# Last two experts of a mixture layer added as late rows, three weight loads in flight to the end, bookkeeping at another place

## The chip, the cores and the metric

One core of one Trainium2 chip runs the kernel. The metric is the device time of one execution in microseconds, as the median of three runs. Engines are named as in the profile: PE (TensorE, PEld its weight loads), DVE (VectorE), ACT (ScalarE), POOL (GpSimd), SP (the engine that here only issues DMAs).

## The reference

One layer of a hybrid backbone on 512 latent tokens and 256 context tokens of width 1024: modulation from a conditioning vector, a bidirectional gated linear attention, and then a grouped top-2 mixture of 16 experts, and a final RMSNorm. The change lies in the last two parts:

```
h2 = modulate(rmsnorm(x, norm2_g), sh2, sc2)           # (512, 1024)
scores = sigmoid(h2 @ w_router);  sel = scores + b_router
best   = group (of 4) with the largest sum of its two largest sel
idx    = the two largest sel inside that group
gates  = one_hot(idx) * scores / (sum of the two scores)
for e in range(16):
    he  = silu(h2 @ w1[e]) * (h2 @ w3[e])              # 1024 -> 512
    out = out + gates[:, e] * (he @ w2[e])             # 512 -> 1024
x = x + g2 * out
return rmsnorm(x, final_g)
```

Every token goes to two experts of one group, so each expert has some of the 512 tokens.

## The kernel before

**Sparse experts.** The kernel counts and ranks the tokens of each expert on the chip. Experts 2 to 15 of its order are sorted by their number of tokens, so that slot 14 and 15 hold the smallest (room for 32 tokens each). Each expert is a tile of tokens: `Tile_` (over 64 tokens, products split in three terms), `Part` for 64 or 32 tokens, where 2 or 4 column groups of the array work side by side on a half or a quarter of the width (`A` = 4 for the last two). The tokens' rows are gathered from DRAM (`h2d`) by indirect DMA on POOL, and an expert's result is added to the rows of `accd` in DRAM by an indirect DMA that accumulates (`scatter`, line 1106). One such scatter waits for the one before it.

**Weights.** An expert's weights are six units of 1 MB: parts a and b (gate and up, line 688) and d (down). `pump` issues them on SP in the order of `queue`, as soon as a buffer is free; `load_unit` also makes each load wait until an earlier one has landed (`back`), which sets how many are in flight: 3, and 2 from the 88th load on and for the two halves of the last unit.

**Order.** The main loop, for i from 0 to 14, does up a of expert i, down of i-1, up b of i, and then the scatter of i-1. Its order on PE, DVE and ACT comes from the scheduler, POOL's is written. The tail (after `finish_consts`) is written out by hand for all engines: down of 14, its scatter, up of 15, reads of `accd` into four tiles of 128 tokens (line 1342), a gather of expert 15's own rows of `accd` (`late_rows`), then squares, norm and output of the four tiles (`finish_half`), the down product of 15, and its rows once more with expert 15's part added (`late_add`, `late_square`, `late_out`), which POOL stores over the output (`late_store`, line 1393).

**Bookkeeping.** A block behind that (`ctx2`, lines 1457 to 1491) works out which experts have more tokens than their room; a loop then treats those (`For_i`, with the number `nblk` read from SBUF). The scheduler may place the block on DVE from the mark of expert 10's store on.

Of the kernel before, what the change touches and what calls it, by code (L numbers as in the profile page):

```python
# [8 lines left out]
F32 = mybir.dt.float32  # L9
# [9 lines left out]
P = 128  # L19
# [13 lines left out]
def dit_kernel(ctx: ExitStack, tc: tile.TileContext, I, out):  # L33
# [647 lines left out]
    def load_unit(u, e, s, hs=None):  # L681
        t = u[s] if s in u else free.pop(0)
        if t is None:
            t = stg.tile([P, 2048], F32, tag="st", name="st")
        w, v = (I[("w_gate_e", "w_up_e")[s % 2]], s // 2) if s < 4 else (I["w_down_e"], s - 4)
        w = w[0, e, v] if isinstance(e, int) else w[0, bass.ds(e, 1), v].rearrange("a p n -> (a p) n")
        h = slice(0, 2048) if hs is None else slice(1024 * hs.start, 1024 * hs.stop)
        d = nc.sync.dma_start(t[:, h], w[:, h])
        if len(dmas) >= 3 and not isinstance(e, int):
            back = 2 if hs is not None or len(dmas) >= 88 else 3  # L690
            tc.add_manual_dep(d.ins, dmas[-back].ins.name, mybir.DependencyInfo(mybir.DependencyClass.Sync, mybir.DependencyReason.DATA), reason="queue depth")
        dmas.append(d)
        u[s] = t
# [488 lines left out]

    class Part:
        def __init__(s, c, w):
            s.idx, s.gs, s.late, s.mark = gix2[:, c:c + 1], gsl[:, c:c + 1], None, None
# [26 lines left out]
        def tr(s):  # L1212
            pt = bank(pb)
            for k in range(s.nk):
                PE.transpose(pt[:, k * P:(k + 1) * P], s.he[:, k * P:(k + 1) * P], ident)
            pt = pt[:, 0:s.n].rearrange("p (k a t) -> p k a t", k=s.nk, a=s.A)
            s.hr = s.he[:, 0:s.n // 2].rearrange("p (k a t) -> p k a t", k=s.nk, a=s.A // 2)
            S.activation(s.hr, pt[:, :, 0:s.A // 2], AF.Silu)
            V.tensor_mul(s.hr, s.hr, pt[:, :, s.A // 2:s.A])
            s.py = bank()[:, 0:s.n]  # L1220

        def dn(s, kt, w):
# [90 lines left out]
    one = raw2[0:1, :]  # L1313
    ss3, rstd3 = R("ss3", [4]), R("rstd3", [4])
    fin = {}

    def finish_consts():
        f, e = free.pop(0), free.pop(0)
        fin["g"], fin["j"], fin["row"] = f[:, 0:1024], f[:, 1024:2048], f[0:1, 1024:2048]
        fin["y"], fin["z"] = [[u[:, h * 1024:h * 1024 + 1024] for u in (free.pop(0), free.pop(0)) for h in range(2)] for _ in range(2)]  # L1320
        fin["h"], fin["g2"], fin["y15"] = [e[:, k * 512:k * 512 + 512] for k in range(3)]
        nc.scalar.dma_start(fin["row"], I["final_g"].rearrange("(o n) -> o n", o=1))
        V.memset(one, 1.0)
# [8 lines left out]
    def finish_g():  # L1332
        for a in range(2):
            sl = slice(a * 512, a * 512 + 512)
            pt = bank()
            PE.matmul(pt, one, fin["row"][:, sl], start=True, stop=True)
            S.copy(fin["g"][:, sl], pt)
        lay("h", fin["g"])
# [5 lines left out]
    def squares(t):  # L1344
        S.activation(fin["j"], fin["y"][t], AF.Square, accum_out=ss3[:, t:t + 1])

    def finish_rsqrt(t):
        rsqrt(rstd3[:, t:t + 2], ss3[:, t:t + 2], 2, 1.0 / D, "a", between=(lambda: finish_mul(3)) if t else None)

    def finish_mul(t):  # L1350
        (V if t % 2 else G).tensor_mul(fin["z"][t], fin["y"][t], fin["g"])

    def finish(t):
        z, r = fin["z"][t], rstd3[:, t:t + 1]
        V.tensor_scalar(z, z, r, None, op0=OP.mult)
# [12 lines left out]
    QA = P // tiles[-1][2]
    SELP = wr.rearrange("p k e -> p (k e)")
# [4 lines left out]
    lrs = R("lrs", [1])  # L1374

    def late_rows(t):
        t.z = xbuf()[:, 0:t.n]
        gather(t.z, parts(accd, t.A), t.idx, t.A * T)

    def late_add(t):  # L1380
        V.tensor_add(t.z, t.z, t.y)

    def late_square(t):
        S.activation(mo.tile([P, 512], BF16, tag="ohx", name="jk3", bufs=NO)[:, 0:t.n], t.z, AF.Square, accum_out=lss)

    def late_out(t):
# [34 lines left out]
    with tc.manual_schedule(engines=tail):  # L1421
        p_, q_ = ex[NE - 2:]
        p, q = p_.tls[0], q_.tls[0]
        p.late = mo.tile([P, D], F32, tag="t4", name="y", bufs=NY)[:, 0:p.n]
        q.late = fin["y15"][:, 0:q.n]
# [6 lines left out]
        for c in "uFab":  # L1432
            if c == "F":
                finish_load()
            elif c in "0123":
                finish_load([int(c)])
            else:
                load_unit(wts[NE - 1], regs[NE - 1], {"u": 4}.get(c, 5), {"a": range(1), "b": range(1, 2)}.get(c))
        late_rows(q)
        q_.turn()  # L1440
        S.preload_act_table_set("natural_log_exp_and_others")
        for h in range(2):
            finish_half(2 * h)
# [32 lines left out]
    t64 = big2[:, 0:64]  # L1476
    for x in range(NB):
        V.scalar_tensor_tensor(t64, cr, float(x + 1), capb.rearrange("p b e -> p (b e)"), op0=OP.is_equal, op1=OP.mult)
        V.tensor_reduce(off[:, x:x + 1], t64, axis=AX.X, op=OP.add)
        V.tensor_scalar(t64, cr, float(x + 1), None, op0=OP.is_equal)  # L1480
        V.tensor_reduce(ohe[:, x], t64.rearrange("p (b e) -> p e b", b=4), axis=AX.X, op=OP.add)
        ob = ohe[:, x].unsqueeze(1).to_broadcast([P, 4, NE])
        V.tensor_mul(tmp4.rearrange("p (t e) f -> p t (e f)", t=4), zm, ob)
        V.tensor_reduce(pmo[:, x], tmp4.rearrange("p (t e) f -> p t (e f)", t=4), axis=AX.X, op=OP.add)
        V.tensor_mul(tmp4.rearrange("p (t e) f -> p t (e f)", t=4), oh[:, 1], ob)
        V.tensor_reduce(k1o[:, x], tmp4.rearrange("p (t e) f -> p t (e f)", t=4), axis=AX.X, op=OP.add)
# [53 lines left out]
```

## Time and profile before

| | us |
|---|---|
| median of 3 runs (654.6 to 658.16) | 656.12 |
| the profiled execution | 656.5 |
| its span | 654.7 |
| busy PE / DVE / ACT / POOL | 599.0 / 463.6 / 302.6 / 98.3 |
| DMA traffic | 168.41 MB, mean 257 GB/s |

The profiled execution is one more run, 0.4 us above the median; the span goes from its first to its last instruction. Times in the rows are counted from the start of the span. A DMA's issue and its landing are two things: the row of the issuing engine shows the issue alone.

### The profile page before, as it was taken

Reading aid. Unit: us, or ns where it says so; the run is one execution under the profiler, and the core shown is the slowest. Engines: PE = TensorE matmul, PEld = TensorE weight load, DVE = VectorE, ACT = ScalarE, POOL = GpSimd, SP = SyncE. Lnnn points to the kernel's source line nnn. Section 1 sums busy time; section 2 is a strip of 40 time slices with the busy share of each in tenths; the row PEclk is TensorE's granted clock in tenths of the full one; section 3 lists DMA queues with packets and bytes.
Section 4 is the critical chain, followed back from the end, with each engine's and each line's share of the span. In section 5 each row is a group of like instructions: output and inputs, shape, how many; then the busy total and the mean of one; then the engine's idle time right before and its main releaser. Section 6 shows DMA issues by size and latency. Waiting matters only on the chain. (4 is left out here: it accounts for less than half of the span.)

```text
span 654.7 us, 11203 instructions
## 1 busy us (share of the span) xinstructions
PE 599.0 (91%) x4200; PEld 412.4 (63%) x4200; DVE 463.6 (71%) x984; ACT 302.6 (46%) x511; POOL 98.3 (15%) x102
## 2 busy tenths in 40 slices
PE   3999999999999999999979989999999999999741
PEld 2778577776878878778748465545565657664310
DVE  5667499849985972575288399465767689999615
ACT  6433399257352233642451255334444457773131
POOL 4030000010100010012200330120322222222032
PEclk9999999999999999999998999999999999999975
DMA  8996472220234861658662989899999999999974
GB/s 269 340 353 218 175 274 66 67 66 4 67 130 158 270 232 51 254 183 354 237 227 74 373 316 366 326 342 351 412 387 395 362 352 358 393 383 345 298 273 189
DMA packets 50251, 168.41 MB, mean 257 GB/s; under 512 B 6779, under 2 KB 17237, under 8 KB 37138
## 3 DMA queue, kind: packets, MB, share of 16 engines
q1 hardware_dynamic: 43216, 156.26, 64.4%
q0 software_dynamic: 5024, 8.70, 5.6%
q10 hardware_dynamic: 1954, 2.71, 1.3%
q8 instruction: 34, 0.56, 0.3%
q14 instruction: 23, 0.19, 0.1%
HBM read 158.64 MB, written 12.30 MB: 261 GB/s over the span
## 5 line engine op out<-in xcount | busy, mean ns | idle before, releaser
L51 PE MATMUL bk<-wh,fh 128*128 128x512 f32 (+3 forms) x276 | 110.9, 409 | 0.7 <-ACT fh L56 0.4
L52 PE MATMUL bk<-wl,fh 128*128 128x512 f32 (+3 forms) x276 | 111.3, 405 | 0.0
L53 PE MATMUL bk<-wh,fl 128*128 128x512 f32 (+3 forms) x276 | 109.0, 399 | 0.5 <-DVE fl L57 0.5
L282 DVE TENSOR_TENSOR wl<-st,wh 128x512 fp32r<-128x512 f32 x60 | 39.9, 685 | 38.9 <-ACT wh L281 37.6
L56 ACT CAST wh<-su 128x1024 fp32r<-128x1024 f32 x45 | 46.8, 1047 | 39.9 <-PE bk L53 38.7
L281 ACT CAST wh<-st 128x512 fp32r<-128x512 f32 x60 | 35.9, 620 | 59.5 <-PE bk L53 50.8
L51 PEld LDWEIGHTS bk<-wh,fh 128*128 128x128 f32 (+3 forms) x276 | 50.2, 183 | 19.2 <-ACT wh L56 3.3
L57 DVE TENSOR_TENSOR wl<-su,wh 128x1024 fp32r<-128x1024 f32 x45 | 54.5, 1222 | 10.5 <-ACT wh L56 8.3
L1106 POOL DMA_INDIRECT accd<-y,gix x16 | 37.2, 2324 | 164.8 <-DVE y L1166 78.2
L52 PEld LDWEIGHTS bk<-wl,fh 128*128 128x128 f32 (+3 forms) x276 | 50.6, 183 | 16.5 <-issue 3.3
L53 PEld LDWEIGHTS bk<-wh,fl 128*128 128x128 f32 (+3 forms) x276 | 50.6, 183 | 13.7 <-issue 1.2
L1202 PE MATMUL bk<-su,he 128*64 128x512 f32 (+1 forms) x136 | 21.7, 526 | 12.5 <-DMA su<-in_w_down_e_dram 9.6
L1202 PE MATMUL bk<-su,xg 128*32 128x256 f32 (+1 forms) x216 | 31.7, 485 | 1.5 <-DVE xg L1196 1.5
L56 ACT CAST fx<-su 128x1024 fp32r<-128x1024 f32 x21 | 22.0, 1050 | 21.8 <-PE bk L53 21.6
L57 DVE TENSOR_TENSOR fx<-su,fx 128x1024 fp32r<-128x1024 f32 x21 | 25.7, 1222 | 7.4 <-ACT fx L56 7.2
L51 PE MATMUL bk<-fx,fh 128*128 128x512 f32 (+3 forms) x68 | 27.9, 410 | 1.2 <-ACT fh L56 1.2
L52 PE MATMUL bk<-fx,fh 128*128 128x512 f32 (+3 forms) x68 | 27.3, 402 | 1.0 <-DVE fx L57 1.0
L53 PE MATMUL bk<-fx,fl 128*128 128x512 f32 (+3 forms) x68 | 26.6, 394 | 0.2 <-DVE fl L57 0.2
L1102 POOL DMA_INDIRECT xg<-h2d,gix x16 | 20.1, 1259 | 39.2 <-DVE pis L1005 15.1
L250 POOL DMA_DIRECT2D mrd<-mrow x8 | 3.8, 487 | 129.2 <-DVE mrow L248 129.2
L1202 PEld LDWEIGHTS bk<-su,he 128*64 128x64 f32 (+1 forms) x136 | 6.6, 127 | 24.4 <-DMA su<-in_w_down_e_dram 11.0
L57 DVE TENSOR_TENSOR fl<-bk,fh 128x512 fp32r<-128x512 f32 (+3 forms) x25 | 15.5, 634 | 7.5 <-ACT fh L56 5.5
(476 smaller groups left out, 1303.6 us busy)
## 6 DMA issues: line engine op xcount, KB each, us to landing
su<-in_w_up_e_dram SPq DMA_DIRECT2D x23, 1024.0 KB, 8.2
su<-in_w_down_e_dram SPq DMA_DIRECT2D x21, 1024.0 KB, 7.8
su<-in_w_gate_e_dram SPq DMA_DIRECT2D x19, 1024.0 KB, 8.3
st<-in_gla_w_in_dram SPq DMA_DIRECT2D x10, 1024.0 KB, 5.0
QQ<-in_w_mod_dram SPq DMA_DIRECT2D x5, 1024.0 KB, 10.8
st<-in_w_gate_e_dram SPq DMA_DIRECT2D x5, 1024.0 KB, 6.8
st<-in_w_up_e_dram SPq DMA_DIRECT2D x5, 1024.0 KB, 9.0
B<-in_w_mod_dram SPq DMA_DIRECT2D x4, 1024.0 KB, 5.1
```

Of the source, the lines that this page charges most:

```text
L51: PE.matmul(o, ah, bh, start=first, stop=False)
L52: PE.matmul(o, ah, bl, start=False, stop=False)
L53: return PE.matmul(o, al, bh, start=False, stop=last)
L56: S.copy(hi, full)
L57: return V.tensor_sub(lo, full, hi.bitcast(F32))
L250: G.dma_start(mrd[4 * h_ + c4:4 * h_ + c4 + 1, :], mrow[32 * c4:32 * c4 + 1, :])
L281: S.copy(w[0][:, k], st[:, k])
L282: mark[0] = V.tensor_sub(w[1][:, k], st[:, k], w[0][:, k].bitcast(F32))
L1102: G.indirect_dma_start(out=xg, out_offset=None, in_=src, in_offset=bass.IndirectOffsetOnAxis(ap=idx, axis=0), bounds_check=n - 1, oob_is_e ...
L1106: G.indirect_dma_start(out=dst, out_offset=bass.IndirectOffsetOnAxis(ap=idx, axis=0), in_=y, in_offset=None, bounds_check=n - 1, oob_is_er ...
L1202: PE.matmul(o[s.w * a:s.w * a + s.w], l, r(a), start=first, stop=last, tile_position=(0, s.w * a))
```

## The change

Six things are edited. (1) `back` is 3 everywhere. (2) Expert 14 is no longer scattered into `accd`: both 14 and 15 are late. `late_consts` makes two one-hot matrices (`hot`: which token of the four tiles stands in which row of the expert) and two matrices of equal numbers (`same`: which rows of the one expert are the same token as which rows of the other). `late_rows` picks the rows of `accd` out of the four tiles by products with `hot`, and `late_other` adds the other expert's share by a product with `same`. Both experts' rows are then normed and stored. (3) The final gain is loaded as a broadcast to 128 partitions, not as one row spread by two products. (4) An output tile is one fused DVE operation (`finish_out`), and POOL does no product. (5) Expert 15's gate uses Exp and a reciprocal (`by_exp`), so that the table is loaded earlier. (6) The bookkeeping may start at expert 4's mark, and its nine steps are done three at a time.

```diff
-            back = 2 if hs is not None or len(dmas) >= 88 else 3
+            back = 3
...
+            gate, up = pt[:, :, 0:s.A // 2], pt[:, :, s.A // 2:s.A]
+            if s.by_exp:
+                S.activation(s.hr, gate, AF.Exp, scale=-1.0)
+                V.tensor_scalar(s.hr, s.hr, 1.0, None, op0=OP.add)
+                V.reciprocal(s.hr, s.hr)
+                V.tensor_mul(s.hr, s.hr, gate)
...
-        nc.scalar.dma_start(fin["row"], I["final_g"].rearrange("(o n) -> o n", o=1))
+        nc.scalar.dma_start(fin["g"], I["final_g"].rearrange("(o n) -> o n", o=1).partition_broadcast(P))
...
-            PE.matmul(pt, one, fin["row"][:, sl], start=True, stop=True)
-            S.copy(fin["g"][:, sl], pt)
...
-    def finish_mul(t):
-        (V if t % 2 else G).tensor_mul(fin["z"][t], fin["y"][t], fin["g"])
-
-    def finish(t):
-        z, r = fin["z"][t], rstd3[:, t:t + 1]
-        V.tensor_scalar(z, z, r, None, op0=OP.mult)
+    def finish_out(t):
+        z = fin["y"][t]
+        V.scalar_tensor_tensor(z, z, rstd3[:, t:t + 1], fin["g"], op0=OP.mult, op1=OP.mult)
         nc.sync.dma_start(out[0, t * P:(t + 1) * P, :], z)
...
-    def late_rows(t):
-        t.z = xbuf()[:, 0:t.n]
-        gather(t.z, parts(accd, t.A), t.idx, t.A * T)
...
+    def late_consts(ts):
+        c = NTL - 2
+        V.tensor_copy(key, gix2[:, c:c + 2])
+        for k in range(2):
+            for t in range(4):
+                V.tensor_scalar(fin["hot"][k][:, t], iot[:, 0:32], zp[:, t, ND - 2 + k:ND - 1 + k], None, op0=OP.is_equal)
+            pt = bank(pb)[:, 0:P]
+            PE.transpose(pt, key[:, k:k + 1].to_broadcast([P, P]), ident)
+            V.tensor_scalar(fin["same"][k], pt, key[:, 1 - k:2 - k], None, op0=OP.is_equal)
+
+    def late_rows(ts, k):
+        for i, t in enumerate(ts):
+            if k == 0:
+                t.rows, t.z = bank()[:, 0:t.n], fin["late"][2 + i]
+            t.groups(t.rows, fin["hot"][i][:, k], lambda a: fin["y"][k][:, a * t.n:a * t.n + t.n], k == 0, k == 3)
+
+    def late_other(ts, i):
+        pt = bank()[:, 0:ts[i].n]
+        PE.matmul(pt, fin["same"][i], ts[1 - i].y, start=True, stop=True)
+        return pt
...
+        G.drain()
+        late_consts(pq)
         p_.down(wts[NE - 2])
-        p_.scatter()
-        G.drain()
-        finish_g()
+        S.preload_act_table_set("natural_log_exp_and_others")
         q_.up(wts[NE - 1], "a")
+        load_unit(wts[NE - 1], regs[NE - 1], 4)
+        finish_load()
+        for h in range(2):
+            load_unit(wts[NE - 1], regs[NE - 1], 5, range(h, h + 1))
+        S.copy(fin["late"][3], late_other(pq, 1))
         q_.up(wts[NE - 1], "b")
...
+        for k in range(2, 4):
+            squares(k)
+            late_rows(pq, k)
+        finish_scale(2)
+        lay("h", fin["g"])
+        V.tensor_add(p.z, p.y, p.rows)
+        V.tensor_add(q.z, q.z, q.rows)
+        finish_out(2)
         q_.down(wts[NE - 1])
-        late_add(q)
-        late_square(q)
-        late_out(q)
-        late_store(q)
+        V.tensor_add(q.z, q.z, q.y)
+        V.tensor_add(p.z, p.z, late_other(pq, 0))
+        finish_out(3)
+        late_out(pq)
...
-    ctx2.enter_context(tc.issue_after(ex[10].mark.ins))
+    ctx2.enter_context(tc.issue_after(ex[4].mark.ins))
```

On SP, before, the end of the weight loads and the reads of `accd`, with what each waits for (DMAHW and DMASW are landings of DMAs of SP or ACT and of POOL, by lanes; `su` and `st` are weight buffers, `B` and `su_2692` take the rows of `accd`):

```order
L688 DMA su_2700<-in_w_gate_e_dram 128x2048 [waits DMAHW6_49,PE_49]
L688 ISA
L688 DMA su_2693<-in_w_up_e_dram 128x2048 [waits DMAHW7_49,PE_49]
L688 ISA
L688 DMA st<-in_w_gate_e_dram 128x2048 [waits DMAHW2_49,DMAHW0_49,DVE_49]
L688 ISA
L688 DMA st<-in_w_up_e_dram 128x2048 [waits DMAHW3_49,DMAHW1_49,DVE_49]
L688 ISA
L688 DMA su_2698<-in_w_down_e_dram 128x2048 [waits DMAHW2_49,PE_49]
L1342 DMA B_86<-accd 128x1024 [waits DMASW7_49,DMASW6_49,DMASW0_49]
```

The same place on SP now:

```order
L688 DMA su_2700<-in_w_gate_e_dram 128x2048 [waits DMAHW5_49,PE_49]
L688 ISA
L688 DMA su_2693<-in_w_up_e_dram 128x2048 [waits DMAHW6_49,DMAHW1_49,PE_49]
L688 ISA
L688 DMA st<-in_w_gate_e_dram 128x2048 [waits DMAHW7_49,DVE_49]
L688 ISA
L688 DMA st<-in_w_up_e_dram 128x2048 [waits DMAHW0_49,DVE_49]
L688 ISA
L688 DMA su_2696<-in_w_down_e_dram 128x2048 [waits DMAHW1_49,PE_49]
L1341 DMA B_86<-accd 128x1024 [waits DMASW7_49,DMASW6_49,DMASW4_49]
```

Each load waits for the landing of the third load before it, not the second; the load into `su_2693` also waits for lane DMAHW1, on which the gain's broadcast stands; the read of `accd` waits for the scatters of 11 to 13, not for one of 14 (lane DMASW0).

On POOL, before, from the scatters of experts 12, 13 and 14 on:

```order
L1106 DMA accd<-y,gix 512x1024 [waits DMASW4_49,DVE_49]
L1106 DMA accd<-y,gix_3326 1024x512 [waits DMASW6_49,DVE_49]
L1106 DMA accd<-y,gix_3326 2048x256 [waits DMASW7_49,DVE_49]
L1102 DMA xg<-accd,gix_3326 128x256 [waits DMASW1_49,DMASW0_49,PE_49]
L1351 TENSOR_TENSOR su_2696<-B_86,srg 128x1024 [waits DMAHW6_49,DMAHW5_49,DMAHW7_49,DMAHW1_49,Activation_49]
L1351 TENSOR_TENSOR su_2697<-su_2692,srg 128x1024 [waits DMAHW3_49,DMAHW7_49,DMAHW0_49,PE_49]
L1393 DMA out_dram<-xg,gix_3326 2048x256 [waits DMAHW5_49,DMAHW4_49,DMAHW6_49,DMAHW3_49,DVE_49]
```

And now:

```order
L1102 DMA xg<-h2d,gix_3326 128x256 [waits DMASW7_49,PE_49]
L1106 DMA accd<-y,gix 512x1024 [waits DMASW4_49,DVE_49]
L1106 DMA accd<-y,gix_3326 1024x512 [waits DMASW6_49,DVE_49]
L1401 DMA out_dram<-srg,gix_3326 2048x256 [waits DMAHW5_49,DMAHW4_49,DMAHW6_49,DMAHW3_49,DVE_49]
L1401 DMA out_dram<-srg,gix_3326 2048x256 [waits DMASW1_49,DMASW0_49,DVE_49]
```

The third scatter, the gather and the two products are gone; there are two late stores, and the second waits for lane DMASW0, which is that of the first.

On DVE, now, from the second pair of output tiles' norm to the end (`srg` holds the constants and late rows, `lrs` the late rows' norms):

```order
L1458 TENSOR_TENSOR srg<-srg,bk 128x256 [waits PE_49]
L1459 TENSOR_TENSOR srg<-srg,bk 128x256 [waits PE_49]
L1351 SCALAR_TENSOR_TENSOR su_2692<-su_2692,rstd_3377,srg 128x1024 [waits DMAHW7_49,DMAHW0_49,DVE_49]
L1234 SCALAR_TENSOR_TENSOR srg<-bk,gsl,srg 128x256 [waits PE_49]
L1462 TENSOR_TENSOR srg<-srg 128x256 [waits DVE_49]
L1463 TENSOR_TENSOR srg<-srg,bk 128x256 [waits PE_49]
L1351 SCALAR_TENSOR_TENSOR su_2692<-su_2692,rstd_3377,srg 128x1024 [waits DMAHW0_49]
L136 TENSOR_SCALAR rsv<-bk 128x2 [waits PE_49]
```

Before, all four output tiles stood ahead of expert 15's store (line 1227), and one add (line 1381) behind it; now the fourth tile is behind it, and so are two adds.

## Rows read from the trace of the kernel before

**Rows 1.** Stretches: us; busy PE, PEld, DVE, ACT, POOL (instructions); clock, DMA share, GB/s.
```profile
460.00:480.00 20.00, 19.10 (x93) 10.96 (x92) 14.69 (x34) 8.66 (x11) 4.93 (x4) 1.00 1.03 407
...
600.00:615.00 15.00, 13.04 (x105) 5.28 (x107) 14.38 (x81) 2.58 (x6) 1.46 (x1) 1.00 0.91 308
615.00:632.00 17.00, 12.53 (x130) 5.25 (x122) 1.60 (x5) 5.36 (x11) 3.12 (x2) 0.90 0.78 257
632.00:655.00 23.00, 2.75 (x18) 0.91 (x18) 11.16 (x21) 6.46 (x16) 7.27 (x4) 0.51 0.60 226
```
**Rows 2.** Timeline of SP, 540 to 655 us: start, us, what was issued.
```profile
545.43 0.33 SPq L688 DMA_DIRECT2D su<-in_w_gate_e_dram  x1
...
593.84 0.33 SPq L688 DMA_DIRECT2D su<-in_w_up_e_dram  x1
601.43 2.80 SPq L688 DMA_DIRECT2D su<-in_w_down_e_dram  x2
...
624.46 0.33 SPq L688 DMA_DIRECT2D su<-in_w_down_e_dram  x1
630.26 2.03 SPq L1342 DMA_DIRECT2D B<-accd  x2
...
633.45 1.09 SPq L688 DMA_DIRECT2D su<-in_w_down_e_dram  x2
```
**Rows 3.** SP's waits, 560 to 655 us: total us, times, longest.
```profile
SPq L688 <- DMA su<-in_w_gate_e_dram: 14.5, 4, 7.0
...
SPq L1342 <- DMA accd<-y,gix: 5.4, 2, 4.9
...
SPq L1494 <- DMA out_dram<-xg,gix: 1.6, 1, 1.6
```
**Rows 4.** Timeline of POOL, 560 to 655 us; in brackets the idle time before, and releaser.
```profile
615.39 1.56 POOL L1106 DMA_INDIRECT accd<-y,gix  x1 [11.41 <-DVE y L1233]
626.01 1.56 POOL L1106 DMA_INDIRECT accd<-y,gix  x1 [9.06 <-DMA accd<-y,gix]
```
**Rows 5.** Line 1106 alone: 400 to 600, 614 to 626, 625.9 to 631 us.
```profile
DMA to landing us min/median/max: 6.5/9.7/14.3
...
DMA to landing us min/median/max: 9.9/9.9/9.9
...
DMA to landing us min/median/max: 4.2/4.2/4.2
```
**Rows 6.** Timeline of all engines, 625 to 655 us.
```profile
634.11 1.06 ACT L1345 ACTIVATE srg<-B 128x1024 f32<-128x1024 f32 x1 [2.43 <-issue]
...
638.35 2.31 DVE L136 TENSOR_SCALAR rsv<-ss 128x2 f32<-128x2 f32 x1
...
640.10 0.30 ACT L139 ACTIVATE rsl<-ss,epsc 128x2 f32<-128x2 f32 x1
...
642.51 1.08 PE L1202 MATMUL bk<-su,he 128*32 128x256 f32 x8 [0.74 <-DMA su<-in_w_down_e_dram]
...
645.74 0.48 DVE L1227 SCALAR_TENSOR_TENSOR srg<-bk,gsl,srg 128x256 f32<-128x256 f32 x1
646.25 0.42 DVE L1381 TENSOR_TENSOR xg<-xg,srg 128x256 f32<-128x256 f32 x1
...
647.03 0.19 ACT L1384 ACTIVATION_READ_ACCUMULATOR jk<-xg 128x1 f32 x1
...
649.20 0.48 DVE L1390 SCALAR_TENSOR_TENSOR xg<-xg,lrs,srg 128x256 f32<-128x256 f32 x1
649.98 1.06 POOL L1393 DMA_INDIRECT out_dram<-xg,gix  x1 [9.35 <-DVE xg L1390]
```
**Rows 7.** Timeline of PE, 615 to 632 us.
```profile
618.99 1.98 PE L1336 MATMUL bk<-srg,raw 1*128 1x512 f32 x4
```
**Rows 8.** The page's costliest groups: shapes, count, busy us, mean ns, idle before.
```profile
L57 DVE TENSOR_TENSOR wl<-su,wh 128x1024 fp32r<-128x1024 f32 x45 | 54.5, 1222 | 10.5 <-ACT wh L56 8.3
```
**Rows 9.** DMA issues, 596 to 655 us: count, KB each, us to landing.
```profile
out_dram<-su SPq DMA_DIRECT2D x4, 512.0 KB, 3.0
```

More of the change, by code (lines that the diff above doesn't have):

```diff
@@ L1217, in tr @@
             s.hr = s.he[:, 0:s.n // 2].rearrange("p (k a t) -> p k a t", k=s.nk, a=s.A // 2)
-            S.activation(s.hr, pt[:, :, 0:s.A // 2], AF.Silu)
-            V.tensor_mul(s.hr, s.hr, pt[:, :, s.A // 2:s.A])
+            gate, up = pt[:, :, 0:s.A // 2], pt[:, :, s.A // 2:s.A]
[4 more added lines that the diff above has]
+                V.tensor_mul(s.hr, s.hr, gate)
+            else:
+                S.activation(s.hr, gate, AF.Silu)
+            V.tensor_mul(s.hr, s.hr, up)
             s.py = bank()[:, 0:s.n]
@@ L1318, in finish_consts @@
         f, e = free.pop(0), free.pop(0)
-        fin["g"], fin["j"], fin["row"] = f[:, 0:1024], f[:, 1024:2048], f[0:1, 1024:2048]
-        fin["y"], fin["z"] = [[u[:, h * 1024:h * 1024 + 1024] for u in (free.pop(0), free.pop(0)) for h in range(2)] for _ in range(2)]
-        fin["h"], fin["g2"], fin["y15"] = [e[:, k * 512:k * 512 + 512] for k in range(3)]
-        nc.scalar.dma_start(fin["row"], I["final_g"].rearrange("(o n) -> o n", o=1))
-        V.memset(one, 1.0)
+        fin["g"], fin["j"] = f[:, 0:1024], f[:, 1024:2048]
+        fin["y"] = [u[:, h * 1024:h * 1024 + 1024] for u in (free.pop(0), free.pop(0)) for h in range(2)]
+        fin["h"], fin["g2"], *fin["late"] = [e[:, k * 256:k * 256 + 256] for k in range(6)]
+        fin["hot"] = [e[:, 1536 + 128 * k:1664 + 128 * k].rearrange("p (t s) -> p t s", t=4) for k in range(2)]
+        fin["same"] = [e[:, 1792 + 128 * k:1920 + 128 * k] for k in range(2)]
+        nc.scalar.dma_start(fin["g"], I["final_g"].rearrange("(o n) -> o n", o=1).partition_broadcast(P))
         lay("g2", g2b)
@@ L1373, in dit_kernel, with late_out @@
         V.tensor_add(sv, sv, ia) if a else V.tensor_copy(sv, ia)
-    lrs = R("lrs", [1])
-    def late_rows(t):
-        t.z = xbuf()[:, 0:t.n]
-        gather(t.z, parts(accd, t.A), t.idx, t.A * T)
[L1380 to L1386, printed above, removed]
-        pt = bank(pb)
-        PE.matmul(pt[:, 0:1], SELP, lss, start=True, stop=True)
-        rsqrt(lrs, pt[:, 0:1], 1, 1.0 / D, "x")
-        V.scalar_tensor_tensor(t.z, t.z, lrs, fin["h"][:, 0:t.n], op0=OP.mult, op1=OP.mult)
+    lrs, lsq, key = R("lrs", [2]), m1[:, 2:4], m1[:, 0:2]
+    def late_consts(ts):
[16 more added lines that the diff above has]
+        return pt
+    def late_out(ts):
+        for i, t in enumerate(ts):
+            S.activation(mo.tile([P, 512], BF16, tag="ohx", name="jk3", bufs=NO)[:, 0:t.n], t.z, AF.Square, accum_out=lsq[:, i:i + 1])
+        pt = bank(pb)
+        PE.matmul(pt[:, 0:2], SELP, lsq, start=True, stop=True)
+        rsqrt(lrs, pt[:, 0:2], 2, 1.0 / D, "x")
+        for i, t in enumerate(ts):
+            V.scalar_tensor_tensor(t.z, t.z, lrs[:, i:i + 1], fin["h"][:, 0:t.n], op0=OP.mult, op1=OP.mult)
+            late_store(t)
     def late_store(t):
@@ L1423, in dit_kernel @@
         p, q = p_.tls[0], q_.tls[0]
[L1424 to L1425 removed]
+        p.late, q.late = fin["late"][0:2]
+        q.by_exp = True
+        pq = (p, q)
+        G.drain()
+        late_consts(pq)
         p_.down(wts[NE - 2])
[L1427 to L1429 removed]
+        S.preload_act_table_set("natural_log_exp_and_others")
         q_.up(wts[NE - 1], "a")
[L1431 to L1443 removed]
+        load_unit(wts[NE - 1], regs[NE - 1], 4)
[3 more added lines that the diff above has]
+        S.copy(fin["late"][3], late_other(pq, 1))
+        q_.up(wts[NE - 1], "b")
+        q_.turn()
+        for k in range(2):
+            squares(k)
+            late_rows(pq, k)
+        finish_scale(0)
+        for k in range(2):
+            finish_out(k)
+        for k in range(2, 4):
+            squares(k)
+            late_rows(pq, k)
+        finish_scale(2)
[3 more added lines that the diff above has]
+        finish_out(2)
         q_.down(wts[NE - 1])
[L1445 to L1448 removed]
+        V.tensor_add(q.z, q.z, q.y)
+        V.tensor_add(p.z, p.z, late_other(pq, 0))
+        finish_out(3)
+        late_out(pq)
     ctx2 = ExitStack()
[L1452 removed]
+    ctx2.enter_context(tc.issue_after(ex[4].mark.ins))
     NB = 9
@@ L1475, in dit_kernel @@
     pmo, k1o = [f.rearrange("p (x t) -> p x t", x=NB) for f in (sc.rearrange("p t e -> p (t e)")[:, 0:4 * NB], big2[:, 512 - 4 * NB:512])]
[L1476 to L1486, printed above, removed]
+    NX3 = 3
+    for x in range(0, NB, NX3):
+        xs = slice(x, x + NX3)
+        bx = big2[:, 0:64 * NX3].rearrange("p (x n) -> p x n", x=NX3)
+        bt = big2[:, 0:64 * NX3].rearrange("p (x t e) -> p x t e", x=NX3, t=4)
+        wide = lambda a, n: a.unsqueeze(1).to_broadcast([P, NX3] + n)
+        V.scalar_tensor_tensor(bx, wide(cr, [64]), -1.0, iof[:, xs].unsqueeze(2).to_broadcast([P, NX3, 64]), op0=OP.add, op1=OP.is_equal)
+        V.tensor_reduce(ohe[:, xs], bx.rearrange("p x (b e) -> p x e b", b=4), axis=AX.X, op=OP.add)
+        V.tensor_mul(bx, bx, wide(capb.rearrange("p b e -> p (b e)"), [64]))
+        V.tensor_reduce(off[:, xs], bx, axis=AX.X, op=OP.add)
+        for dst, src in ((pmo, zm), (k1o, oh[:, 1])):
+            V.tensor_mul(bt, wide(src, [4, NE]), ohe[:, xs].unsqueeze(2).to_broadcast([P, NX3, 4, NE]))
+            V.tensor_reduce(dst[:, xs], bt, axis=AX.X, op=OP.add)
     V.tensor_mul(big2[:, 0:NB * NE].rearrange("p (x e) -> p x e", x=NB), ohe, iof.unsqueeze(1).to_broadcast([P, NB, NE]))
@@ L1498, in dit_kernel @@
         index_of(0, [(0, 0, P)], lambda e_: pmx, lambda e_: rv[:, :, 0])
+        p.scatter()
         q.scatter()
-        V.tensor_scalar(gix2[:, NTL - 1:NTL], gix2[:, NTL - 1:NTL], 2 * q.A * T, None, op0=OP.add)
+        V.tensor_scalar(gix2[:, NTL - 2:NTL], gix2[:, NTL - 2:NTL], 2 * q.A * T, None, op0=OP.add)
         o, u = Expert([(0, P)]), {}
```

21 lines of the change are left out of this document (6 added, 15 removed).

## The prediction

> **What bounds the kernel now.** I read the table of stretches first. From 440 to 600 us TensorE and the DMA engines are both full, as in 460 to 480 us: PE busy 19.10 of 20, DMA share 1.03, 407 GB/s. From 600 us both sag: 308 GB/s, then 257 with PE busy 12.53 of 17 [rows 1]. An edit ahead of 600 us pays only if it frees both, one behind it pays where the chain to the end runs; so I read the timeline of the DMA-issuing engine (SP) next, to see why the DMA sags.
>
> Up to 593.84 us SP issues one 1 MB weight load every 2.85 us: 18 loads from 545.43 to 593.84, three in flight. From load 88 on the kernel holds the depth at 2. The next load goes 7.6 us later, at 601.43, and from there to 624.46 seven loads go, one every 3.8 [rows 2]. The last half of the last expert's weights is issued only at 633.45, behind the four reads of accd, whose first goes at 630.26.
>
> Why 630.26? The list of SP's waits says that the read of accd waited for scatters into accd (two waits, 4.9 us the longer) [rows 3]. There are two in a row: expert 13's, on POOL at 615.39, and expert 14's, which could start only at 626.01 because it waits for the first [rows 4]. The landings of the scatter's own line say how long each took: 9.9 us the first (landed 625.3), 4.2 the second (landed 630.2, which is when SP goes on) [rows 5]. So the end is set by: product of expert 13, scatter 13, scatter 14, read of accd (call its start A = 630.26), then reads and weights, final norm, a late store, end.
>
> The rest of the tail from that A, by the timeline [rows 6]: first square at A+3.85, the last norm's Ln at A+9.84, last down product at A+12.25 (642.51, 1.08 long), VectorE takes it up only at 645.74 because it is still busy with the output tiles (one of its tiny operations took 2.31 us at 638.35, beside POOL's 1024-wide product), late store on POOL at 649.98 = A+19.72. It lands about 652.6, 1.6 after the issue's end [rows 3]; the branch and barriers end the span at 654.7.
>
> **The change part by part.**
> *Expert 14's scatter goes* (its rows are now added late). A then waits for scatter 13 alone. When is that issued? TensorE's order ahead of expert 13's down product gains two key transposes, and VectorE loses the bookkeeping that stood there: eight kinds of small operation, nine of each. The hidden layer of 13 is ready when ScalarE's Silu is; the bookkeeping cost it about 0.4 us of queueing and the two transposes with their VectorE comparison give that back. I leave the issue at 615.3. Its landing is 9.9 us beside two loads; under depth 3, from 400 to 600 us, the same line shows 6.5 / 9.7 / 14.3 (least, median, most) [rows 5]. I take 9.7, the median under the depth that will hold: A = 625.0, a gain of 5.3. Ends: 4.2 (alone) gives 619.5, 14.3 gives 629.6.
>
> *Depth 3 to the end.* SP's 7.0 us wait for a gate load [rows 3] ended with the landing of expert 14's second gate load, right before 601.43. The load behind it lands about 2.85 later, near 604; seven more, the last of them the first half of expert 15's down weights, take until 604 + 7 x 2.85 = 624, and the 0.5 MB broadcast of the final gain, new on ScalarE's queue, adds half a load, 1.4: about 625.4. Before, that load was issued at 624.46. The second load of expert 15 waits for that broadcast (lane DMAHW1 in the order); two loads are in flight meanwhile, so I price it at 0, and at up to 2.85 if they run out. So weights and scatter are both there at about 625, and neither gains much from more of the other. After A, nothing in the weights' queue waits: the last half's issue was 3.2 behind A and stays so.
>
> The Trainium skill (page "DMA: Bandwidth & Descriptors", section "Queues, rings and completion order") says that each DMA engine takes turns between the queue rows that have work, packet by packet. By that a third load in SP's row does not push POOL's scatter back by a whole load; the rows above (median 9.7 under depth 3, 9.9 under depth 2) agree, and the slow rival below loses chance by it.
>
> *The gather of accd rows goes; one-hot products and four accd reads replace it.* 32 products of 256 columns on TensorE, which is busy 2.75 of 23 us there [rows 1]: hidden behind the landing of the reads; the last eight stand behind the last read (about A+8.4), and eight such products took 1.08 [rows 6]. Cost 0, as the down weights land later. The table load moves into idle ScalarE time, and the Exp form of the gate adds three small VectorE operations where VectorE idles. Cost 0; were the cover gone they are under 1 us. The two K=1 products of the gain (1.98) [rows 7] leave a place that also waited for weights: 0.
>
> *The end chain on VectorE and ScalarE.* Squares and norms have the loads' times: norm of the second pair ready at A+10.4. One fused operation per output tile replaces a product and a scaling; a 128x1024 two-input VectorE operation costs 1.22 (row of line 57) [rows 8], and POOL's products, beside which VectorE's were slow, are gone. VectorE: polish to A+11.1, two adds of 0.42, third output tile to A+13.2. The last product ends at about A+13.1, so VectorE takes it up at A+13.2, not A+15.5 as before: 2.3 gained. Then new work: store 0.48, add 0.42; the product with the equal-number matrix, full width: two of 512 columns took 1.98 at clock 1.00 [rows 7], so 256 cost 0.5, and 1.0 at half of it, 1.2 GHz; the end of the span had a granted clock of 0.51 [rows 1], so I take 1.0; add 0.42; fourth output tile 1.22, its issue at A+16.6; squares, sum and norm of both experts, one square (0.6) longer. From the end of the square to the scaled row it took 2.46 [rows 6]; so the first late row is ready at about A+19.2, and the fourth tile's landing, 3.0 after its issue [rows 9], which the store also waits for, at A+19.6. Against A+19.72: -0.1, with -1.1 to +1.2 as ends.
>
> *Two late stores instead of one.* In POOL's order the second store waits for DMASW0, the lane of the first: both write the output. The first took 2.6 from start to landing (1.06 of issue and 1.6) [rows 3, 6], so the second starts and lands 2.6 + 0.2 later: +2.8. If it had only to be issued behind the other it would be 1.06.
>
> By the same page, section "Anatomy of one DMA — SWDGE (gpsimd) path", a POOL DMA costs 2.0 us plus bytes over 436 GB/s, an estimate of 2.3 for the 128 KB here; the sum would be 0.3 lower, and the rows' 2.6 decides.
>
> *Bookkeeping from 590 us to about 450 to 498 us, 72 small operations to 24 wider ones.* VectorE is busy 14.69 of 20 there [rows 1], so some 9 us of it fit into idle time in two such stretches; a weight split that comes late behind one costs TensorE, which has 0.9 idle. I take 0; ends -0.5 (the waits at 595 to 610 gone) and +3 (a third of it on TensorE).
>
> **Sum.** -5.3 (A) -0.1 (chain) +2.8 (second store) +0 = -2.6. On the profiled execution, 656.5 with its span of 654.7: 653.9. That execution lies 0.4 above the median of 656.12, so 653.5 for the median.
>
> **The rivals.**
> 1. The queue is nearly empty when scatter 13 runs, and it lands in 6 to 7 us, A = 622. For it: alone it takes 4.2, and 6.5 has been seen under load. Against: by the pace of 2.85 the weights are in flight until 625. -8.3 - 0.1 + 2.8 = -5.6: 650.5.
> 2. The deeper queue holds the scatter. With 14.3, which the line showed once under depth 3, A = 629.6; with the second store the sum is -0.7 - 0.1 + 2.8 = +2.0: 658.1. It decides from A = 627.6 on. For it: two late stores in series cost 2.8 whatever else happens. Against: the median of 9.7.
> 3. The moved bookkeeping stalls TensorE between 450 and 498 us, where it has no slack; a delay there is carried through scatter 13 to the end. +3 on the sum: 656.5. For it: PE busy 19.10 of 20 there. Against: VectorE's idle 5 of 20, and splits that are made a step ahead.
>
> **How the numbers follow.** Forecast 50%: 653.5, itself between 651.6 and 655.4 (ends of the chain's price and of A by one microsecond). Rival 1 25%, rival 2 12%, rival 3 13%. A measurement can tell 0.5%, 3.3 us: under 652.8 or over 659.4. Faster: all of rival 1 and 0.35 of the forecast, 0.43. Slower: half of rival 2 and half of rival 3 with their tails, 0.12. The same: 0.45. The range reaches from past rival 1, 649, to rival 2, 658.5.
>
> **What would show it.** Right: SP's weight issues at 2.6 to 3 us up to expert 15's down half, at 613 to 617; the first accd read at 624 to 626, released by a scatter; VectorE's store of the last product right behind PE's end; two stores on POOL at the end, 2.7 to 3 us apart. Wrong: an accd read at or past 628, or at 622; stores one right behind the other; PE waits for VectorE's line 57 between 450 and 500 us that add up to over 1 us; a last store starting later than A+20.5.

## The result, and the profile after

The change makes the kernel slower: 661.5 us as the median of eight runs, against 656.05 for the kernel before beside it; the ratio is 1.0083, with a 95% interval of 1.0064 to 1.0102, or +5.4 us. (Seven runs lie between 660.5 and 664.5; the eighth was disturbed, at a granted clock of 0.65, and is not in the ratio.) The profiled execution took 660.54 with a span of 658.7, 4.0 more than the span before.

The stretches of the changed kernel, columns as in [rows 1], with one stretch more where the bookkeeping now stands:

```profile
460.00:480.00 20.00, 18.99 (x92) 10.87 (x91) 16.38 (x47) 8.59 (x10) 5.67 (x4) 1.00 0.99 375
480.00:500.00 20.00, 19.98 (x87) 11.07 (x86) 18.21 (x39) 8.59 (x11) 4.25 (x3) 1.00 1.02 387
...
600.00:615.00 15.00, 14.13 (x91) 5.66 (x93) 4.97 (x16) 2.58 (x6) 1.46 (x1) 1.00 0.91 337
615.00:632.00 17.00, 10.64 (x152) 4.93 (x144) 4.14 (x9) 3.80 (x7) 1.57 (x1) 1.00 0.96 351
632.00:655.00 23.00, 7.68 (x92) 3.50 (x84) 9.41 (x23) 7.51 (x22) 2.07 (x2) 0.65 0.45 172
```

Up to 600 us TensorE's busy time has hardly changed: from 480 to 500 us VectorE is busy 18.21 of 20 (12.90 before), and TensorE 19.98 in both kernels. But equal busy time is not equal progress. On POOL, the scatters of experts 5 and 7 now:

```profile
482.94 2.31 POOL L1106 DMA_INDIRECT accd<-y,gix  x1 [7.80 <-DVE y L1166]
...
516.10 2.29 POOL L1106 DMA_INDIRECT accd<-y,gix  x1 [9.74 <-DVE y L1166]
```

and before:

```profile
482.92 2.31 POOL L1106 DMA_INDIRECT accd<-y,gix  x1 [9.56 <-DVE y L1166]
...
515.08 2.29 POOL L1106 DMA_INDIRECT accd<-y,gix  x1 [9.64 <-DVE y L1166]
```

So 1.0 us is lost between the two, where the bookkeeping now stands, and it stays (expert 12's scatter goes at 603.52 against 602.52). TensorE's order differs there. Now two matmuls of a down product stand apart from the other 14:

```profile
491.26 1.07 PE L1202 MATMUL bk<-su,he 128*64 128x512 f32 x2
...
493.63 3.65 PE L1202 MATMUL bk<-su,he 128*64 128x512 f32 x14
```

and before all 16 stood together:

```profile
494.33 3.65 PE L1202 MATMUL bk<-su,he 128*64 128x512 f32 x16
```

From 600 to 632 us the DMA engines carry more than before (337 and 351 GB/s against 308 and 257), and the first read of accd goes 4.0 us sooner (626.25 against 630.26). So the rest of the loss, and the larger part, lies behind that read.

SP's timeline of the changed kernel answers to [rows 2]:

```profile
605.63 0.34 SPq L688 DMA_DIRECT2D su<-in_w_gate_e_dram  x1
614.64 0.33 SPq L688 DMA_DIRECT2D su<-in_w_up_e_dram  x1
...
619.65 0.33 SPq L688 DMA_DIRECT2D su<-in_w_down_e_dram  x1
626.25 0.81 SPq L1341 DMA_DIRECT2D B<-accd  x2
...
639.78 3.14 SPq L1352 DMA_DIRECT2D out_dram<-su  x2
```

and SP's waits to [rows 3] (total us, times, longest):

```profile
SPq L688 <- DMA srg<-in_final_g_dram: 8.5, 1, 8.5
...
SPq L1341 <- DMA accd<-y,gix: 6.2, 1, 6.2
```

The first read of accd, A, goes at 626.25, released by a scatter as forecast (625.0). But SP stood still from 605.63 to 614.64, and the wait is for the gain's broadcast: 8.5 us, which the forecast priced at nothing, or up to 2.85. The table of DMA issues gives that broadcast 10.2 us from issue to landing:

```profile
srg<-in_final_g_dram ACTq DMA_DIRECT2D x1, 512.0 KB, 10.2
```

POOL's timeline, for [rows 4], has one scatter at the end and two late stores:

```profile
616.57 1.57 POOL L1106 DMA_INDIRECT accd<-y,gix  x1 [11.59 <-DVE y L1240]
646.24 1.05 POOL L1401 DMA_INDIRECT out_dram<-srg,gix  x1 [28.10 <-SPq L1513]
649.43 1.02 POOL L1401 DMA_INDIRECT out_dram<-srg,gix  x1 [2.14 <-issue]
```

and scatter 13's landing, for [rows 5]:

```profile
DMA to landing us min/median/max: 9.6/9.6/9.6
```

The tail by the timeline of all engines, for [rows 6]:

```profile
631.15 1.06 ACT L1344 ACTIVATE srg<-B 128x1024 f32<-128x1024 f32 x1 [1.93 <-DMA B<-accd]
...
636.45 0.30 ACT L139 ACTIVATE rsl<-ss,epsc 128x2 f32<-128x2 f32 x1
...
639.67 0.48 DVE L1234 SCALAR_TENSOR_TENSOR srg<-bk,gsl,srg 128x256 f32<-128x256 f32 x1
...
640.20 0.70 PE L1387 MATMUL bk<-srg 128*128 128x256 f32 x2 [1.49 <-DVE srg L1234]
...
644.17 0.88 DVE L1397 SCALAR_TENSOR_TENSOR srg<-srg,lrs 128x256 f32<-128x256 f32 x2
```

The second store's last byte has landed by about 652.3 (it took 2.8 from its start). Before, the span ended 4.7 us behind the start of the last store (649.98, [rows 6], to 654.7). Now it ends 9.3 behind it, at 658.7, with no engine busy. What stands there is seen only among the sequencers' own instructions, by the last line of the program. Now (duration in ns: least, median, most; first and last start):

```profile
L1556 SPq DRAIN  x3: 7/7/13, 653.0 to 658.2; - x3
L1556 POOLq DRAIN  x3: 52/105/4723, 653.2 to 658.5; - x3
```

and before:

```profile
L1536 SPq DRAIN  x3: 7/7/13, 653.4 to 654.2; - x3
L1536 POOLq DRAIN  x3: 46/105/212, 653.6 to 654.4; - x3
```

The first of POOL's three last drains, 0.21 us before, takes 4.72 us: from 653.2 to 657.9, and the end follows. The kernel has a drain of its own, `G.drain()`. Before, it ran in the tail (line 1428), 7.17 us long and beside other work:

```profile
L1428 POOLq DRAIN  x1: 7168/7168/7168, 625.8 to 625.8; - x1
```

Now the line stands ahead of `late_consts` with nothing to wait for, and the scheduler put it at the front of the program:

```profile
L1435 POOLq DRAIN  x1: 7363/7363/7363, 5.2 to 5.2; - x1
```

There it hides too, but 57 POOL DMAs stand behind it in POOL's order, where before 2 stood (the gather and the late store). The count needs care: POOL's issues in the trace show 61 and 3 records that start later than the drain's own start, but 4 and 1 of these start while the drain still runs, and belong to DMAs that stand ahead of it. Run e1 below shows this: its drain is held behind scatter 13, yet the drain's record starts at 616.44 and the scatter's at 616.68.

### The profile page after: what moved, and what is told of

The parts are those of the page before. It is cut to its first block, busy times and chain, and to the rows that moved or that the text cites. A ratio compares the mean times of both kernels' runs of the same rounds, so it can differ in the third digit from the quotient of the medians.

```text
span 658.7 us, 11293 instructions
## 1 busy us (share of the span) xinstructions
PE 603.8 (92%) x4266; PEld 415.1 (63%) x4266; DVE 463.1 (70%) x951; ACT 302.1 (46%) x512; POOL 89.8 (14%) x99
## 5 line engine op out<-in xcount | busy, mean ns | idle before, releaser
L1106 POOL DMA_INDIRECT accd<-y,gix x15 | 34.3, 2290 | 157.9 <-DVE y L1166 86.8
L56 ACT CAST fx<-su 128x1024 fp32r<-128x1024 f32 x21 | 22.0, 1049 | 21.9 <-PE bk L53 21.7
L52 PE MATMUL bk<-fl,wh 128*128 128x512 f32 x48 | 19.8, 412 | 0.0
L53 PE MATMUL bk<-fh,wl 128*128 128x512 f32 x48 | 19.7, 411 | 0.0
## 6 DMA issues: line engine op xcount, KB each, us to landing
QQ<-in_w_mod_dram SPq DMA_DIRECT2D x5, 1024.0 KB, 10.2
```

Of the source, the lines that this page charges most:

```text
L52: PE.matmul(o, ah, bl, start=False, stop=False)
L53: return PE.matmul(o, al, bh, start=False, stop=last)
L56: S.copy(hi, full)
L1106: G.indirect_dma_start(out=dst, out_offset=bass.IndirectOffsetOnAxis(ap=idx, axis=0), in_=y, in_offset=None, bounds_check=n - 1, oob_is_er ...
```

## The experiments

Theory D: the program's last drain takes long when many POOL DMAs lie behind the last drain before it; the moved `G.drain()` is the loss. Its rivals: the moved bookkeeping, the deeper queue, and the broadcast that holds up SP (theory B). The ratios are to the kernel before, run on the same chip in the same rounds.

**The drain at the end again (e1).** The changed kernel, its drain held behind scatter 13:

```diff
-        G.drain()
+        with tc.issue_after(ex[NE - 3].tls[-1].sc.ins):
+            G.drain()
```

> The changed kernel, with one edit: POOL's drain instruction stands behind expert 13's scatter (in the changed kernel it had moved to 5 us, and the last drain of the program took 4.72 us, against 0.21 before). Theory D (a drain behind many indirect DMAs costs about 5 us once, and the change moved it from a hidden place to the end): the drain at about 617 us takes 5 to 7 us and hides nothing on the path, the last one falls to about 0.2, and the time falls by 4 to 5 us, from 661.5 to about 657, the kernel before's 656.05 within 2 us. Theory R (the last drain is long because of the two late stores just ahead of it, wherever another drain stands): the last drain stays at 4 to 5 us and the time at 660 to 662.

Measured: 657.78 us, ratio 1.0008 (0.9991 to 1.0024). Against the changed kernel's ratio of 1.0083 that is 0.75%, or 4.9 us (4.3 between the medians, each taken against its own runs of the kernel before). Its own drain is hidden in the tail, 12.48 us long, and the last is short, although two late stores stand just ahead of it (theory R):

```profile
L1436 POOLq DRAIN  x1: 12481/12481/12481, 616.4 to 616.4; - x1
```

```profile
L1557 POOLq DRAIN  x3: 52/105/218, 656.6 to 657.4; - x3
```

**No drain in the kernel before (e2).**

```diff
-        G.drain()
```

> The kernel before, without the drain instruction behind expert 14's scatter. Theory D: its last drain grows from 0.21 us to about 4.7, and the time from 656 to about 660, although it has one late store and none of the other edits; the gather behind the drain may start a little earlier. Theory R: the last drain stays at 0.2 and the time at 656, or under it by what the drain of 7.17 us held up.

Measured: 661.67 us, ratio 1.0071 (1.0046 to 1.0097), so +4.7, or +5.0 between the medians, on a kernel that has nothing else of the change. Its last drain:

```profile
L1535 POOLq DRAIN  x3: 46/105/5540, 653.2 to 659.3; - x3
```

The drain alone makes the kernel before as slow as the changed one, and giving it back its place takes the loss away. Theory D is shown from both sides.

**The drain five experts earlier (e8).** A single run, of 660.62 us, of which only the trace is used:

```diff
+        with tc.issue_after(ex[8].tls[-1].sc.ins):
+            G.drain()
```

> As e1, but POOL's drain stands behind expert 8's scatter, some 100 us earlier, with the scatters and gathers of five more experts behind it. Theory D1 (the last drain's length grows with the number of POOL's transfers since the one before): it takes between e1's 0.22 us and the changed kernel's 4.72, by the share of transfers left some 1 us. Rival D2 (a drain is short only when few transfers, or none still under way, lie since the last): 0.2 us or the full 4.7.

Measured: with 11 POOL DMAs between the two drains the last takes 0.95 us, as D1 expected:

```profile
L1557 POOLq DRAIN  x3: 52/105/952, 657.1 to 658.6; - x3
```

It is neither short nor full: it grows with the count. Together with e6 below (1 DMA, 0.13 us), the kernel before and e1 (2, 0.21 and 0.22), the changed kernel (57, 4.72) and e2 (67, 5.54), that is 0.082 us for each POOL DMA since the drain before, over some 0.05, and all six lie within 0.01 us of that line. The time since the drain before does not do it: it is 27.8 us in the kernel before (0.21), 33.4 in e6 (0.13) and 40.1 in e1 (0.22). Nor do bytes or packets: from e8 to the changed kernel the DMAs behind the drain grow 5.2 times (11 to 57), and so does the drain above its 0.05, but what POOL's queue moves behind it grows 3.5 times in bytes (2.46 to 8.49 MB) and 4.5 times in packets (1024 to 4592).

**The bookkeeping back at expert 10 (e3), depth 2 at the end (e4).** Both on e1:

```diff
-    ctx2.enter_context(tc.issue_after(ex[4].mark.ins))
+    ctx2.enter_context(tc.issue_after(ex[10].mark.ins))
```

> The first kernel of this set with the bookkeeping (in its three wider steps) allowed from expert 10's mark again instead of expert 4's. In the changed kernel's trace scatters from 500 us on are about 1.0 us later than before. If the moved bookkeeping is the cause, that 1 us goes: the scatter of expert 13 about 1 us earlier than in the first kernel, the time 0.5 to 1 us lower. If it is not, the time stays within 0.5 us of the first kernel, or is higher because the bookkeeping stands ahead of expert 13's product.

```diff
-            back = 3
+            back = 2 if hs is not None or len(dmas) >= 88 else 3
```

> The first kernel of this set with the old rule of depth (2 from the 88th load on). If depth 3 is what brings the read of accd and the last weights early, the first accd read and the last down weights come 2 to 4 us later and the time rises by 2 to 4. If the scatter alone sets the read of accd (my prediction's term), the read starts within 1 us of the first kernel's and the time changes by under 1 us.

Measured: e3 657.23, ratio 1.0011 (0.9994 to 1.0029); e4 658.33, ratio 1.0013 (0.9994 to 1.0032). Neither can be told from e1. The traces do tell the two places of the bookkeeping apart: from expert 5's scatter to expert 7's is 33.1 to 33.2 us in all eight kernels that have it at expert 4 (the changed one, e1, e4 to e6, e8, e9, e11), and 32.2 in all five that have it at expert 10 (the one before, e2, e3, e7, e10); only the first eight split the down product on TensorE. e1 and e3 differ in the place alone, as do e9 and e10, so the place costs 1.0 us at that point. Scatter 13 goes at 615.48 in e3's profiled run (the fastest of its twelve) and at 616.68 in e1's (the slowest). How much of that 1.0 us reaches the end, the medians cannot tell.

**Depth 3 in the kernel before (e7).** The first line of the change alone.

> The kernel before with queue depth 3 to the end and nothing else. By e4 (depth 2 put back at the end of e1: nothing measurable) no difference: 656.6, within 0.3%. Rival: before, with expert 14's scatter still in the chain, the earlier weights do show, or the deeper queue holds scatters 13 and 14: 2 us either way.

Measured: 656.64, ratio 0.9990 (0.9973 to 1.0007): nothing. SP's timeline says why:

```profile
616.78 0.33 SPq L688 DMA_DIRECT2D su<-in_w_down_e_dram  x1
629.23 0.81 SPq L1342 DMA_DIRECT2D B<-accd  x2
```

The weights are issued 7.7 us sooner (624.46 before, [rows 2]), yet the reads of accd wait for two scatters as before, 629.23 against 630.26.

**The gain as a row again (e5).** On e1, the broadcast undone:

```diff
-        nc.scalar.dma_start(fin["g"], I["final_g"].rearrange("(o n) -> o n", o=1).partition_broadcast(P))
+        nc.scalar.dma_start(fin["row"], I["final_g"].rearrange("(o n) -> o n", o=1))
...
+            PE.matmul(pt, raw2[0:1, :], fin["row"][:, sl], start=True, stop=True)
+            S.copy(fin["g"][:, sl], pt)
```

> The changed kernel with the drain behind scatter 13 (as in e1), and the final gain loaded as one 4 KB row and spread by two products, as before, in place of the 0.5 MB broadcast. Theory B (the broadcast holds up SP: in e1 a weight load of expert 15 waits on its lane from about 608 to 615.3 us, and expert 15's first down half lands only at 630.9): that wait goes, SP's loads run on at 2.6 to 3 us apart, the first down half lands at 625 to 627, the last read of accd within 8.5 us of the first, and the time is 3 us or so under e1: 655. Rival theory C (the wait is hidden, two other loads being in flight, and the end is set by scatter 13 and the chain behind the first read): the loads move, the first read of accd stays at 626 and the first late store 20 us or more behind it: 657.5 to 658, ratio within 0.2% of e1's.

SP's timeline of e1 shows the stop, from 607.75 to 615.30:

```profile
607.75 0.34 SPq L688 DMA_DIRECT2D su<-in_w_gate_e_dram  x1
615.30 0.33 SPq L688 DMA_DIRECT2D su<-in_w_up_e_dram  x1
...
622.29 0.33 SPq L688 DMA_DIRECT2D su<-in_w_down_e_dram  x1
```

and that of e5 the loads running on, the first down half issued 5.8 us sooner:

```profile
604.00 0.34 SPq L688 DMA_DIRECT2D su<-in_w_gate_e_dram  x1
606.49 0.33 SPq L688 DMA_DIRECT2D su<-in_w_up_e_dram  x1
...
616.47 0.33 SPq L688 DMA_DIRECT2D su<-in_w_down_e_dram  x1
```

Measured: 656.07, ratio 0.9990 (0.9966 to 1.0015), 0.18% under e1's, not theory B's 3 us, and inside rival C's 0.2%. The profiled run, the fastest of its twelve (653.39), has what theory B expected; the medians alone do not tell e1 and e5 apart, so the pair was repeated (e11).

**One late store (e6).** On e1, expert 14's rows are not stored:

```diff
-            late_store(t)
+            if i:
+                late_store(t)
```

> As e1, but expert 14's late rows are not stored (the output lacks expert 14's rows): one late store at the end. Theory S (the second store runs wholly behind the first, 3.2 us from start to start): the time falls by 3.2 us, to 654.5. Rival: part of the first store's time is hidden behind the fourth output tile's landing or the last drain, which then becomes the bound: a fall of 1 to 2 us.

Measured: 653.55, ratio 0.9947 (0.9927 to 0.9967), 0.61% or 4.0 us under e1. The two intervals leave some 2 to 6 us, so theory S (all of the second store's 3.2 us counts, none of it hidden) is borne out and the rival's 1 to 2 us are unlikely.

**Expert 14 stored without waiting for 15 (e9, and e10 with the bookkeeping at 10).** Where a token goes to both experts, expert 15's store writes it last and whole, so 14's rows need not hold 15's share. On e5:

```diff
+        late_square(0, p)
         finish_out(2)
+        lay("h", fin["g"])
+        late_out(0, p, between=lambda: finish_out(3))
         q_.down(wts[NE - 1])
         V.tensor_add(q.z, q.z, q.y)
-        V.tensor_add(p.z, p.z, late_other(pq, 0))
-        finish_out(3)
-        late_out(pq)
+        late_square(1, q)
+        late_out(1, q)
```

> As e5 (drain behind scatter 13, gain as a row), but expert 14's late rows no longer wait for expert 15: they are normed and stored right after the four output tiles, without 15's share, and expert 15's store, which goes behind, writes the tokens that both have. So only one late store is left behind expert 15's last product. Theory S (the second store is 3.2 us in series at the end; e6, without it, was some 4 us faster than e1): 14's store starts when the fourth tile has landed, near 641, 15's about 3.2 us later at 643.5 to 644 in place of e5's 646.5, and the time is 3 us under e5's: ratio to before 0.9945, about 653. Rival R (VectorE: the fourth tile and 14's norm now stand ahead of expert 15's rows, so 15's store is later by what the early store gains): 655.5 to 656, ratio 0.998 to 1.000.

> As e9, with the bookkeeping from expert 10's mark on, as before the change. In e1 scatter 13 was issued 1.2 us later than before, and in e3 (the bookkeeping at 10) at before's time, though the medians of e1 and e3 differ by 0.5 us only, within their spread. Theory: what the early bookkeeping costs is at most that 1 us; the time is 0 to 1.2 us under e9's. Rival (its place is worth nothing, and the 1.2 us is the spread from one run to the next): within 0.3 us of e9.

Measured: e9 654.55, ratio 0.9971 (0.9953 to 0.9990); e10 654.48, ratio 0.9963 (0.9948 to 0.9978), beside 657.02 for the kernel before. Both beat it, by 0.3 to 0.4%, some 2 us. That they beat e5 is not shown: e9's ratio lies 0.2% under e5's, not the 3 us expected, and the two intervals overlap. e9's timelines show what holds it. SP:

```profile
638.55 1.59 SPq L1360 DMA_DIRECT2D out_dram<-su  x2
```

and POOL:

```profile
643.31 1.05 POOL L1409 DMA_INDIRECT out_dram<-srg,gix  x1 [25.40 <-DVE rsv L136]
647.22 1.02 POOL L1409 DMA_INDIRECT out_dram<-srg,gix  x1 [2.86 <-issue]
```

Expert 14's rows were scaled at 640.8, but their store waits for the fourth output tile, issued about 639.8 and, by the 2.7 to 3.7 us of the other three, landed between 642.5 and 643.5 (this is the one wait of the store that ends so late; the releaser in the brackets had long been done). 15's store then waits for 14's, 3.9 us from start to start. So the series hangs on the output tile, not on expert 15, and it did so in the changed kernel too, where the late rows were ready at 645.05, the fourth tile was issued at 642.59 and the store went at 646.24. Counted from the first read of accd, the last store starts at 21.9 us in e9 and at 22.0 in e5. The place of the bookkeeping is again worth nothing that can be told at the end (e10 against e9).

**The broadcast in e9 (e11).** The e5 edit, undone:

```diff
-        finish_g()
...
+        nc.scalar.dma_start(fin["g"], I["final_g"].rearrange("(o n) -> o n", o=1).partition_broadcast(P))
```

> As e9 (early store), with the final gain as the 0.5 MB broadcast again. In e1 SP stood from about 608 to 615.3 us waiting for the broadcast, in e5, without it, the loads ran on, but the medians of e1 and e5 (ratios to before 1.0008 and 0.9990) do not tell the two apart. Theory B (that wait costs 1 to 3 us at the end): SP waits to 615 again, and the time is 1 to 3 us over e9's, ratio to before 0.9985 to 1.0015. Rival C (the wait is hidden by the loads in flight): SP waits again and the ratio stays within 0.0015 of e9's 0.9971.

Measured: 657.32, ratio 1.0003 (0.9983 to 1.0022), 0.32% or 2.1 us over e9's. SP waits again:

```profile
604.33 0.34 SPq L688 DMA_DIRECT2D su<-in_w_gate_e_dram  x1
614.60 0.33 SPq L688 DMA_DIRECT2D su<-in_w_up_e_dram  x1
```

With e1 against e5 (1.2 us) the two pairs agree in sign and size: the broadcast costs 1 to 2 us. Each pair's intervals still overlap, so the size is no better known than that. Nor is all of it SP's wait. In both pairs TensorE's order also changes ahead of expert 13's down product, and scatter 13 goes 13.06 us behind scatter 12 with the broadcast and 12.41 with the row. No run tells these 0.65 us from the wait.

## Why the prediction was wrong

Forecast 653.5 in a range of 649.0 to 658.5; measured 661.5. The step that failed is the sum itself, -5.3 - 0.1 + 2.8 + 0: it took everything behind the last store's start as it was, and so put one moved instruction at nothing without a reason. `G.drain()` stands in the diff at its old and its new place, but it has no term in the prediction. It cost 4.5 us in the profiled run, and e1 and e2 show it from both sides (4.9 and 4.7). By the profiled executions, in the order of the prediction:

- **A.** Forecast 625.0, measured 626.25: +1.25 on the sum. The landing was right (9.6, taken 9.7); the issue of scatter 13 came at 616.57, not 615.3, and 1.0 of that is the moved bookkeeping. The first rival (A at 622) and the second (629.6) did not come true.
- **The end chain.** From A to the first late store 19.99 us, forecast 19.62: +0.4. The pieces fit: VectorE took up the last product at A+13.4 (forecast A+13.2), the product with equal numbers took 0.70 (forecast 1.0), the late rows were ready at A+18.8 (A+19.2), and the fourth tile, which the store waited for as forecast, was issued at A+16.3 (A+16.6). The store started 3.65 behind that, not 3.0.
- **The second late store.** 3.19 from start to start, forecast 2.8: +0.4. The series was right (2.14 us of idle POOL between the two), its price a little low; e6 finds it at the end. One of the signs of being wrong was set wrong itself: "a last store starting later than A+20.5" would speak against the forecast's own last store, at A+22.4 (19.6 and 2.8); it measured A+23.2.
- **From the last store's start to the end of the span.** 9.27, taken at before's 4.72: +4.55. This is the drain, 4.72 instead of 0.21.

The four make 6.6; with -2.6 that is +4.0, the difference of the two spans.

The Trainium skill (page "VectorE: DVE Perf Modes", section "The DRAIN you can't avoid") takes the drains of a program's end for some 12 ns each on all engines. The traces agree for SP's, 7 to 13 ns; for the first of POOL's three the rows decide, 0.13 to 5.54 us.

- **Depth 3** was rightly put at nothing (e4, e7), though for the kernel before the reason is that the reads wait for scatters.
- **The broadcast** was priced at 0 with an upper end of 2.85 "if they run out". They ran out: SP stood 8.5 us, since the 0.5 MB took 10.2 us beside weight loads, not the half load of 1.4 that the prediction gave it, and from 613.7 to 616.6 us the DMA engines carried 112 GB/s (404 in e5). Expert 15's first down half was issued at 619.65, not at 613 to 617. The broadcast's cost, 1 to 2 us (e5, e11; some of it TensorE's order), lies within the end given.
- **The bookkeeping** was put at 0 and cost 1.0 us on the way to scatter 13. The third rival had this path right (a delay on TensorE, carried through scatter 13) and its size, 3, wrong; its sign, waits of TensorE for line 57, is not there: from 450 to 500 us TensorE waits 0.5 and 0.5 us, for other lines, against 0.5 and 0.4 before. What changed is the order. At the end e3 and e10 find nothing that can be told.
- **Products in place of the gather, the Exp gate, the fused tiles** were hidden or as priced, as far as the tail's rows show: the late rows were ready no later than forecast.

So with the drain repaired (e1) the change is worth nothing that can be told (1.0008), not -2.6. The prices found roughly add up to that: A came 4.0 sooner, the later scatter included, against 3.2 for the second store and 1 to 2 for the broadcast. Without the broadcast it is 0.9990, whose interval reaches to 0.9966; the forecast's ratio would be 0.996.

Open is how much of the bookkeeping's 1.0 us reaches the end, and what spreads the runs of one kernel over up to 7.5 us (in the profiled runs scatter 13 goes between 615.4 and 618.8); e5's profiled run, at 653.4, has A at 624.50 and the first late store at A+18.8, but its median lies 2.7 above.

## What to carry to other kernels

Read a diff for the instructions that carry no data, too: a drain that moves from the tail to the front still runs, but what it had taken off the end comes back there. Equal busy time in a stretch does not say that nothing was lost there: find the same instruction in both traces. When no engine is busy at the end of a span, look at the sequencers' own instructions by the program's last line. And price a load by its landing in the queue that it joins: a lane that another queue's next load waits for turned a half-megabyte extra into a stop of 8.5 us here.

## What the runs showed of the hardware

- The first of POOL's three last drains lasts by the number of POOL DMAs since its last drain: 0.13 us after 1, 0.21 and 0.22 after 2, 0.95 after 11, 4.72 after 57, 5.54 after 67, that is 0.05 and 0.082 for each. Why each of them costs this, these runs do not tell.
- A drain in the tail or in mid program takes 7.2 to 13.5 us and holds back what stands behind it on POOL: in e8 a gather that goes at 537.60 in e1 goes at 549.05. It ended 2.3 to 2.7 us behind the landing of the scatter just ahead of it (628.92 and 626.25 in e1). Scatter 13 is none the later for it: e8's scatters are 2.1 us behind e1's ahead of the drain already (501.32 against 499.26) and still at the end (618.76 against 616.68).
- A 0.5 MB broadcast of one row on ScalarE's queue lands 9.3 to 10.7 us after its issue beside weight loads on SP.
- Two indirect stores in series on POOL are 3.2 us apart from start to start, 1.05 of it the issue (3.5 to 3.9 in e9 to e11).
